# Start offsets of SBUF tiles: small tiles move to one filled pool, and every large tile begins at a multiple of 512 bytes

## The chip, the core and the metric

One core of a Trainium2 chip runs the whole layer. The metric is the device time of one execution in microseconds (us). The program is one straight list of instructions for each engine, so every execution issues the same work in the same order.

## What is computed

One layer of a hybrid encoder on x of shape (1, 512, 1024) in float32, with hidden width 2816 in the two feed-forward halves:

```
x = x + 0.5 * swiglu(rmsnorm(x, ffn1_norm_g), ffn1_w_gate, ffn1_w_up, ffn1_w_down)
h = rmsnorm(x, mix_norm_g)
proj = h @ w_in                                   # 1024 -> 3072
y_hy = hyena_mixer(proj[..., :1536], ...)         # gates and two long convolutions
y_at = dilated_attention_mixer(proj[..., 1536:])  # 8 heads of 64
y = concatenate([rmsnorm(y_hy, ...), rmsnorm(y_at, ...)])
x = x + y @ w_out
x = x + 0.5 * swiglu(rmsnorm(x, ffn2_norm_g), ffn2_w_gate, ffn2_w_up, ffn2_w_down)
return rmsnorm(x, final_norm_g)
```

## The kernel before

**The matmuls.** Activations lie transposed in SBUF: 128 channels on the partitions, the 512 tokens along each partition. So a tile of 128x512 float32 takes 2048 bytes of each partition, and a block of weights of 128x128 takes 512. To keep float32 accuracy at the rate of the type float32r, each operand is split in a high part, rounded to float32r, and a low part, the rest. `mm3` then issues three matmuls for each block, at lines 146, 147 and 148: high times high, high weights times low activations, low weights times high activations. The weights are the stationary operand, the 512 tokens the moving one. Where float32 itself is multiplied (transposes with `ident`, the products of the attention weights with v, the sums over `ones`), a matmul leaves two records in the trace.

**The tiles by name.** Weights arrive in `wr` by DMA (128x1024, 4096 bytes of each partition), ScalarE (ACT) rounds them to `wh` (line 188) and VectorE (DVE) subtracts to `wl` (line 194). The moving operand is `xh`, `xl` for gate and up (output `pgu`), for the input projections (`pp`), and the stationary one for v (`pv`, where `wh`, `wl` move); `gh`, `gl` for the down projection (`pd`); the tiles named `yg` for the output projection (`pw`). Some early projections take their weights from tiles named `we` instead of `wh`. The filters use `ftabh`, `ftabl` as stationary and `fh`, `fl` as moving operand (`pf`); the Hyena part uses `zh`, `zl` against `ftab` (`pfw`) and `Sh`, `Sl` against `itab` (`pbk`) at 256 columns each.

**The order.** Stages follow each other: FFN 1 (with the filter work woven in, to about 402 us), the mixer (projections, Hyena, attention, output projection, to about 670 us), FFN 2. Inside a stage, streams of work with planned costs are merged by the class `Merge` into one fixed order. Weights are loaded two blocks ahead by SP's queue.

**Where tiles lie.** A pool takes a stretch of each partition, and its tiles stand in it in the order of their first use, each tag times its number of buffers. Every tile is padded to a multiple of 32 bytes. Pools opened with `side="right"` are stacked down from the top. In the built program x0 begins at byte 16512 of the partition, that is 32 x 512 + 128. Counting on from there gives, modulo 512:

| tiles | pool | start modulo 512 |
|---|---|---|
| x0 to x7 | wp | 128 |
| ones | wp | 0 |
| wr, wh, wl, ident, xh, xl, ssq, sq, rb | wp, after cols, eps, ones and warm | 32 |
| z, u, gh, gl; ur, zh, zl, X (yg among them), Sh, Sl | f1, f2; m1, after std and rc | 160 |
| we, qk, v, yh; ftab, itab; fh, fl and most filter tiles | mid; tp; fl (right side) | 480 |

Here cols takes 352 bytes, eps and warm 32 each, and the two buffers each of std and rc take 128 together. The right side ends 32 bytes below the end of the partition.

Of the kernel before, what the change touches and what calls it, by code (L numbers as in the profile page):

```python
# [11 lines left out]
F32 = mybir.dt.float32  # L12
# [6 lines left out]
P = 128  # L19
# [16 lines left out]
NG1, NGM, NGH, NGA, NG2, NGF, NCW, NCB = 0, 8, 16, 20, 24, 32, 40, 76  # L36
NCOL = 88
WR, WB, HQ, SB, UC, ZB, X1B, UR = 2, 3, 3, 3, 3, 3, 3, 3
TWO_PI = 2.0 * math.pi


# [13 lines left out]
def on_p(cost, lag=0.4, **need):  # L55
    return "P", cost, lag, need


def on_v(cost, lag=None, **need):
    return "V", cost, lag, need  # L60


def on_a(cost, lag=0.2, **need):
    return "A", cost, lag, need
# [176 lines left out]
class SumSq:  # L241
# [38 lines left out]
    def rstd_cols(self, n, lag, res, m, ev):  # L280


        g, nc = self.g, self.g.nc
        yield on_v(0.0, lag)
        parts = self.sums()
        yield on_p(0.9 * len(parts), ps=1)
        pc = psum(g, "pc")
        for b in range(4):
            for i, t in enumerate(parts):
                nc.tensor.matmul(pc[:, b:b + 1], t[:, b * P:(b + 1) * P], g.ones[:, 0:1],  # L290
                                 start=i == 0, stop=i == len(parts) - 1)
        yield on_v(0.5, 0.4)
        std = g.wp.tile([P, 4], F32, tag="std", name="std", bufs=2)
        nc.scalar.activation(std, pc[:, 0:4], AF.Sqrt, bias=g.eps, scale=1.0 / n)
        rc = g.wp.tile([P, 4], F32, tag="rc", name="rc", bufs=2)
        nc.vector.reciprocal(rc, std)
        res["rc"] = rc
        m.free(ps=1)
        yield on_p(0.9, ps=1)
        pb = psum(g, "pb")  # L300
        for b in range(4):
            spread(g, pb[:, b * P:(b + 1) * P], rc[:, b:b + 1], P)
        yield on_a(0.7)
        res["rb"] = g.wp.tile([P, S], F32, tag="rb", name="rb", bufs=1)
        nc.scalar.copy(res["rb"], pb)
        m.free(ps=1)
        m.fire(ev)


def spread(g, ps, col, n):  # L310

    g.nc.tensor.matmul(ps, col.to_broadcast([P, n]), g.ident, start=True, stop=True)


def psum(g, name):
    return g.ps.tile([P, S], F32, tag="ps", name=name)
# [85 lines left out]
def split_tab(g, pool, name, src):  # L402
    nc = g.nc
    raw = g.wp.tile([P, 1024], F32, tag="wr", name="tabraw", bufs=WR)
    nc.sync.dma_start(raw, src)
    hi = pool.tile([P, 1024], F32R, tag=name + "h", name=name + "h", bufs=1)
    lo = pool.tile([P, 1024], F32R, tag=name + "l", name=name + "l", bufs=1)
    nc.scalar.activation(hi, raw, AF.Copy)
    nc.vector.tensor_tensor(out=lo, in0=raw, in1=hi.bitcast(F32), op=ALU.subtract)
    return hi, lo  # L410


def sin_layer(g, pool, out, ps, n, b, fr):
# [5 lines left out]
    magic = 12582912.0  # L419
    nc.vector.tensor_scalar(out=t[:n], in0=a[:n], scalar1=1.0 / TWO_PI, scalar2=magic,  # L420
                            op0=ALU.mult, op1=ALU.add)
    nc.vector.tensor_scalar_add(t[:n], t[:n], -magic)
    c1 = 6.28125
    c2 = float(np.float32(np.round((TWO_PI - c1) * 2.0 ** 21) / 2.0 ** 21))
    c3 = float(np.float32(TWO_PI - c1 - c2))
    for c in (c1, c2, c3):
# [7 lines left out]
def filters(g, m, pool, tpool, a, start, done):  # L434
# [3 lines left out]
    yield on_v(2.3, 6.0)  # L438
    g.ftab = split_tab(g, tpool, "ftab", a["ftab"])
    g.itab = split_tab(g, tpool, "itab", a["itab"])  # L440
    fq = pool.tile([P, 4], F32, tag="fq", name="fq", bufs=1)
    nc.sync.dma_start(fq, a["fcol"])
    zt = pool.tile([P, S], F32, tag="fr", name="zt", bufs=1)
# [659 lines left out]
def body(ctx: ExitStack, tc: tile.TileContext, a: dict, out: bass.AP):  # L1103
    nc = tc.nc
    g = Ctx()
    g.nc, g.tc = nc, tc
    pool = lambda n, **k: tc.tile_pool(name=n, bufs=1, **k)
    over = dict(reuse_waits="tile")
    g.ps = ctx.enter_context(tc.tile_pool(name="ps", bufs=8, space=PSUM))
    g.wp = ctx.enter_context(pool("wp"))  # L1110
    dp = ctx.enter_context(pool("dp", space=DRAM))
    g.hdram = [dp.tile([5, 2, P, 2 * CW], F32, tag=f"hd{o}", name=f"hdram{o}") for o in range(2)]
# [2 lines left out]
    n1w = len(f1)  # L1115
    g.w = Weights(g, f1 + mixer_weights(a) + f2)
    g.x = [g.wp.tile([P, S], F32, tag=f"x{d}", name=f"x{d}") for d in range(DT)]
    g.cols = g.wp.tile([P, NCOL], F32, tag="cols", name="cols")
    g.eps = g.wp.tile([P, 1], F32, tag="eps", name="eps")
    nc.vector.memset(g.eps, EPS)  # L1120
    g.ones = g.wp.tile([P, P], F32, tag="ones", name="ones")
    nc.vector.memset(g.ones, 1.0)
    g.warm = warm = g.wp.tile([P, 1], F32, tag="warm", name="warm")
    nc.scalar.activation(warm, g.eps, AF.Silu)
    ps = psum(g, "warm")
    for _ in range(NWARM):
# [5 lines left out]
        if d == 1:  # L1132
            g.w.start()
    g.w.load(1)
    g.ident = g.wp.tile([P, P], F32, tag="ident", name="ident")
    make_identity(nc, g.ident)


# [2 lines left out]
    with pool("f1", **over) as fp:  # L1141
# [29 lines left out]
        st = left.enter_context(pool("st", **over))  # L1171

        m.spawn(filters(g, m, flp, tp, a, nev, fdone), 0.5)
        m.run(until=fdone)
        right2.close()
# [11 lines left out]
    with pool("m1", **over) as hp:  # L1187
# [13 lines left out]
        def squares():  # L1201

            yield wait(at.xev)
            for d in range(DT):
                yield on_v(0.0, 1.4)
                with tc.issue_after(g.rounded.ins):
                    ss2.add(g.x[d])
# [10 lines left out]
    with pool("f2", **over) as fp:  # L1218
        ss3 = SumSq(g)
        n2, nev = {}, Event()  # L1220
        gain = lambda d: g.cols[:, NGF + d:NGF + d + 1]
        sq = {}
        pc = []

        def done2(d):
            ss3.add(g.x[d])
            nc.scalar.activation(g.x[d], g.x[d], AF.Copy, scale=gain(d))
            if d == DT - 4:
                nc.scalar.activation(warm, ss3.acc[:, 0:1], AF.Sqrt)

        def tail(d, th, ps):

            hs = slice(th * CW, (th + 1) * CW)
            x = g.x[d][:, hs]
            if d == DT - 2:
                yield on_p(0.4, 0.0, ps=1)
                pc.append(psum(g, "pc"))
                for b in range(2):
                    bs = slice((2 * th + b) * P, (2 * th + b + 1) * P)
                    nc.tensor.matmul(pc[th][:, b:b + 1], ss3.acc[:, bs], g.ones[:, 0:1],  # L1240
                                     start=b == 0, stop=False)
            yield on_v(0.35)
            nc.vector.scalar_tensor_tensor(out=x, in0=ps[:, 0:CW], scalar=0.5, in1=x,
                                           op0=ALU.mult, op1=ALU.add)
            m.free(ps=1)
            yield on_v(0.0, 0.4)
            sq[d] = g.wp.tile([P, S], F32, tag="sq", name="sq", bufs=2)
            nc.scalar.activation(sq[d][:, 0:CW], x, AF.Square)
            yield on_p(0.3)
            for b in range(2):  # L1250
                nc.tensor.matmul(pc[th][:, b:b + 1], sq[d][:, b * P:(b + 1) * P],
                                 g.ones[:, 0:1], start=False, stop=d == DT - 1 and b == 1)
            if d < DT - 1:
                return
            yield on_v(0.3, 0.6)
            std = g.wp.tile([P, 4], F32, tag="std", name="std", bufs=2)
            nc.scalar.activation(std[:, 0:2], pc[th][:, 0:2], AF.Sqrt, bias=g.eps, scale=1.0 / D)
            rc = g.wp.tile([P, 4], F32, tag="rc", name="rc", bufs=2)
            nc.vector.reciprocal(rc[:, 0:2], std[:, 0:2])
            yield on_p(0.5, 0.2, ps=1)  # L1260
            pb = psum(g, "pb")
            for b in range(2):
                spread(g, pb[:, b * P:(b + 1) * P], rc[:, b:b + 1], P)
            for c in range(DT // 2):
                yield on_v(0.7)
                o = g.wp.tile([P, 2, CW], F32, tag="xh", name="o", bufs=DT)
                for i in range(2):
                    e = 2 * c + i
                    if e < DT - 2:
                        nc.vector.tensor_tensor(out=o[:, i], in0=g.x[e][:, hs], in1=pb[:, 0:CW], op=ALU.mult)  # L1270
                    else:
                        nc.vector.scalar_tensor_tensor(out=o[:, i], in0=g.x[e][:, hs], scalar=gain(e),
                                                       in1=pb[:, 0:CW], op0=ALU.mult, op1=ALU.mult)
                (nc.sync if c % 2 else nc.scalar).dma_start(
                    out[2 * c:2 * c + 2, :, hs].rearrange("d p s -> p d s"), o)
            m.free(ps=2)

        m.spawn(ffn(g, m, fp, at.x2, n2, nev, done2, tail), 1)

        def norm2():  # L1280
            yield from squares()
            yield from ss2.rstd(D, L2, n2, m, nev)

        m.spawn(norm2(), 0)
        m.run()
# [114 lines left out]
```

## Time and profile before

| | |
|---|---|
| median of 3 runs | 1048.6 us (1047.63 to 1049.46) |
| the profiled execution's own time | 1048.07 us |
| its span, first to last instruction | 1046.3 us |
| PE (TensorE matmul) busy | 1032.0 us, 99% of the span |
| DVE (VectorE) busy | 604.5 us, 58% |
| ACT (ScalarE) busy | 402.5 us, 38% |
| mean share of the 16 DMA engines | 33.3% on the main queue |
| granted TensorE clock, mean | 0.995 of 2.4 GHz |

PE's records overlap: a matmul's record lasts 0.39 us, but the next one begins some 0.23 us after it. The pace of a stream of matmuls is therefore read from start to start, or from the number of records in a long stretch, and not from the mean duration of a record.

### The profile page before, as it was taken

The numbers are of one execution on the slowest core, as the hardware profiler recorded it, in microseconds if no ns is written. First come the engines' busy times: TensorE is split into PE (matmuls) and PEld (weight loads), VectorE is DVE, ScalarE is ACT, GpSimd is POOL, SyncE is SP. The second block draws the span as 40 slices with busy tenths as digits, with TensorE's granted clock in tenths as the row PEclk, the third lists the DMA queues.
The fourth block names the chain that finished last, engine by engine and source line by source line (L and its number), as shares of the span: only waits on it lengthen the run. The fifth ranks groups of instructions, "written<-read, shape, count | busy, mean of one in ns | idle before, by whom it ended". The sixth has DMA issues, their size and how long they took to land.

```text
span 1046.3 us, 12667 instructions
## 1 busy us (share of the span) xinstructions
PE 1032.0 (99%) x5012; PEld 844.7 (81%) x5012; DVE 604.5 (58%) x834; ACT 402.5 (38%) x594; POOL 45.9 (4%) x37
## 2 busy tenths in 40 slices
PE   9999999999999999999998999999999999999997
PEld 7877888888888888888886778888888888888886
DVE  5676646554676444887999744764453235444332
ACT  6433432233334332344347874543232213333341
POOL 4000000000000111000000000210000000000010
PEclk9999999999999999999999999999999999999998
DMA  6333423533255222234435311233322332332222
GB/s 216 129 124 106 126 91 118 174 98 104 91 170 171 92 90 91 66 114 143 143 105 186 122 42 61 81 101 101 101 89 93 101 100 86 96 101 101 93 69 81
DMA packets 43513, 114.25 MB, mean 109 GB/s; under 512 B 5082, under 2 KB 12314, under 8 KB 43453
## 3 DMA queue, kind: packets, MB, share of 16 engines
q1 hardware_dynamic: 41644, 111.30, 33.3%
q10 hardware_dynamic: 1808, 2.14, 0.6%
q8 instruction: 39, 0.64, 0.3%
q14 instruction: 22, 0.17, 0.1%
HBM read 106.08 MB, written 7.34 MB: 108 GB/s over the span
## 4 chain that ended last, share of the span: by engine, by line
PE 96%; DVE 2%; ACT 1%; issue 1%; DMA 1%; SPq 0%; DVEq 0%; ACTq 0%
PE pgu L146 15%; PE pgu L147 15%; PE pgu L148 15%; PE pd L146 8%; PE pd L148 8%; PE pd L147 8%; PE pp L146 3%; PE pp L148 3%; PE pp L147 3%; PE pw L146 2%; PE pw L148 1%; PE pw L147 1%; PE po L1008 1%; PE ppt L996 1%; PE pqk L1039 1%; PE pv L146 1%
## 5 line engine op out<-in xcount | busy, mean ns | idle before, releaser
L188 ACT ACTIVATE wh<-wr 128x1024 fp32r<-128x1024 f32 x159 | 168.5, 1060 | 411.9 <-PE pgu L147 143.1
L146 PE MATMUL pgu<-xh,wh 128*128 128x512 f32 x704 | 275.4, 391 | 0.4 <-ACT wh L580 0.4
L147 PE MATMUL pgu<-xl,wh 128*128 128x512 f32 x704 | 274.4, 390 | 0.3 <-DVE xl L236 0.3
L148 PE MATMUL pgu<-xh,wl 128*128 128x512 f32 x704 | 274.5, 390 | 0.1
L194 DVE TENSOR_TENSOR wl<-wr,wh 128x1024 fp32r<-128x1024 f32 x159 | 198.1, 1246 | 114.3 <-ACT wh L188 110.0
L146 PEld LDWEIGHTS pgu<-xh,wh 128*128 128x128 f32 x704 | 132.2, 188 | 31.0 <-issue 2.9
L147 PEld LDWEIGHTS pgu<-xl,wh 128*128 128x128 f32 x704 | 132.1, 188 | 29.6 <-DVE xl L236 1.4
L148 PEld LDWEIGHTS pgu<-xh,wl 128*128 128x128 f32 x704 | 132.1, 188 | 28.3 <-DVE wl L581 0.4
L146 PE MATMUL pd<-gh,wh 128*128 128x512 f32 (+1 forms) x374 | 143.2, 383 | 0.0
L147 PE MATMUL pd<-gl,wh 128*128 128x512 f32 (+1 forms) x374 | 142.7, 382 | 0.0
L148 PE MATMUL pd<-gh,wl 128*128 128x512 f32 (+1 forms) x374 | 142.7, 382 | 0.0
L256 POOL TENSOR_TENSOR ssq<-ssq,sq 128x512 f32<-128x512 f32 x31 | 45.2, 1457 | 975.5 <-ACT sq L252 974.6
L331 DVE TENSOR_TENSOR u<-pgu,rb 128x512 f32<-128x512 f32 x44 | 30.3, 690 | 97.3 <-PE pgu L148 97.3
L147 PEld LDWEIGHTS pd<-gl,wh 128*128 128x128 f32 x374 | 70.3, 188 | 15.1
L148 PEld LDWEIGHTS pd<-gh,wl 128*128 128x128 f32 x374 | 70.3, 188 | 15.0
L146 PEld LDWEIGHTS pd<-gh,wh 128*128 128x128 f32 x374 | 70.3, 188 | 15.0
L329 DVE TENSOR_TENSOR z<-pgu,rb 128x512 f32<-128x512 f32 x44 | 30.4, 691 | 60.6 <-PE pgu L148 60.5
L146 PE MATMUL pp<-xh,wh 128*128 128x512 f32 x128 | 50.0, 391 | 0.0
L147 PE MATMUL pp<-xl,wh 128*128 128x512 f32 x128 | 49.9, 390 | 0.0
L148 PE MATMUL pp<-xh,wl 128*128 128x512 f32 x128 | 49.8, 389 | 0.0
L343 DVE SCALAR_TENSOR_TENSOR x<-pd,x 128x512 f32<-128x512 f32 x30 | 20.7, 690 | 42.7 <-PE pd L148 42.6
L336 ACT ACTIVATE gh<-u 128x512 fp32r<-128x512 f32 x44 | 27.7, 632 | 24.2 <-DVE u L333 23.8
(207 smaller groups left out, 1189.3 us busy)
## 6 DMA issues: line engine op xcount, KB each, us to landing
wr<-w1u SPq DMA_DIRECT2D x22, 512.0 KB, 3.4
wr<-w1d SPq DMA_DIRECT2D x22, 512.0 KB, 3.4
wr<-w2g SPq DMA_DIRECT2D x22, 512.0 KB, 3.4
wr<-w2u SPq DMA_DIRECT2D x22, 512.0 KB, 3.4
wr<-w2d SPq DMA_DIRECT2D x22, 512.0 KB, 3.4
wr<-w1g SPq DMA_DIRECT2D x21, 512.0 KB, 3.4
wr<-win SPq DMA_DIRECT2D x16, 512.0 KB, 3.4
pe<-negb SPq DMA_DIRECT2D x32, 256.0 KB, 3.2
```

The lines of the kernel that those rows point to most:

```text
L146: nc.tensor.matmul(ps, lh, rh, start=start, stop=False)
L147: nc.tensor.matmul(ps, lh, rl, start=False, stop=False)
L148: nc.tensor.matmul(ps, ll, rh, start=False, stop=stop)
L188: self.g.nc.scalar.activation(self.hi[i], self.raw[i], AF.Copy)
L194: self.g.nc.vector.tensor_tensor(out=self.lo[i], in0=self.raw[i], in1=self.hi[i].bitcast(F32), op=ALU.subtract)
L256: g.nc.gpsimd.tensor_tensor(out=self.acc, in0=self.acc, in1=sq, op=ALU.add)
L329: nc.vector.tensor_tensor(out=z, in0=pg, in1=rb, op=ALU.mult)
L331: nc.vector.tensor_tensor(out=u, in0=pu, in1=rb, op=ALU.mult)
L336: nc.scalar.activation(hi, u, AF.Copy)
L343: nc.vector.scalar_tensor_tensor(out=g.x[d], in0=ps, scalar=0.5, in1=g.x[d], op0=ALU.mult, op1=ALU.add)
L996: nc.tensor.transpose(ts[e][:, js], pes[e][:, js], g.ident)
L1008: nc.tensor.matmul(po[e * HD:(e + 1) * HD, b * P:(b + 1) * P], self.mx.v[j][:, h * HD:(h + 1) * HD], tt[e][:, j * P:(j + 1) * P], start=j ...
```

## The change

A new pool `sp` is opened ahead of `wp`, and its first tile is `fill`, 88 float32 on each partition, which nothing writes or reads. The small tiles cols, eps, warm, std and rc move into `sp`. `ident` is allocated right behind `ones`, while the instructions that fill it stay where they were. On the right side, `fillr` (120 float32, also unused) is allocated in `tp` behind the tables.

```
+SMALL = 88
 class SumSq, rstd_cols, and the tail of FFN 2:
-        std = g.wp.tile([P, 4], F32, tag="std", name="std", bufs=2)
+        std = g.sp.tile([P, 4], F32, tag="std", name="std", bufs=2)
-        rc = g.wp.tile([P, 4], F32, tag="rc", name="rc", bufs=2)
+        rc = g.sp.tile([P, 4], F32, tag="rc", name="rc", bufs=2)
 filters:
     g.itab = split_tab(g, tpool, "itab", a["itab"])
+    tpool.tile([P, 120], F32, tag="fill", name="fillr")
 body:
+    g.sp = ctx.enter_context(pool("sp"))
+    g.sp.tile([P, SMALL], F32, tag="fill", name="fill")
     g.wp = ctx.enter_context(pool("wp"))
-    g.cols = g.wp.tile([P, NCOL], F32, tag="cols", name="cols")
-    g.eps = g.wp.tile([P, 1], F32, tag="eps", name="eps")
+    g.cols = g.sp.tile([P, NCOL], F32, tag="cols", name="cols")
+    g.eps = g.sp.tile([P, 1], F32, tag="eps", name="eps")
     g.ones = g.wp.tile([P, P], F32, tag="ones", name="ones")
-    g.warm = warm = g.wp.tile([P, 1], F32, tag="warm", name="warm")
+    g.ident = g.wp.tile([P, P], F32, tag="ident", name="ident")
+    g.warm = warm = g.sp.tile([P, 1], F32, tag="warm", name="warm")
...
-    g.ident = g.wp.tile([P, P], F32, tag="ident", name="ident")
     make_identity(nc, g.ident)
```

Counted out: 16512 + 352 (fill) + 352 (cols) + 32 (eps) + 32 (warm) + 64 (std) + 64 (rc) = 17408 = 34 x 512, where `wp` now begins. `wp` then holds only tiles of whole multiples of 512 bytes, so f1, m1 and f2 begin at such a multiple too; they lie 352 bytes higher than before. On the right side everything lies 480 bytes lower: the tables begin at 212480 = 415 x 512, and `mid` at 179712 = 351 x 512.

## Rows read from the trace of the kernel before

**Rows 1.** The page's first part: busy us, share of the span, instructions.
```profile
PE 1032.0 (99%) x5012; PEld 844.7 (81%) x5012; DVE 604.5 (58%) x834; ACT 402.5 (38%) x594; POOL 45.9 (4%) x37
```

**Rows 2.** Waits of PE: total us, times, longest; first and last of eight.
```profile
PE po L1008 <- ACT pt L1002: 1.9, 1, 1.9
...
PE pgu L147 <- DVE xl L236: 0.3, 1, 0.3
```

**Rows 3.** Stretches: length; busy of PE, PEld, DVE, ACT, POOL (records); clock, DMA share, GB/s.
```profile
10.00:402.00 392.00, 391.77 (x1692) 316.58 (x1693) 234.29 (x295) 147.52 (x196) 18.75 (x13) 1.00 0.38 123
...
500.00:572.00 72.00, 68.92 (x390) 57.20 (x388) 71.28 (x119) 36.12 (x67) 1.27 (x1) 1.00 0.47 149
...
655.00:1022.00 367.00, 367.00 (x1618) 301.30 (x1617) 166.50 (x193) 116.55 (x142) 18.30 (x12) 1.00 0.29 94
```

**Rows 4.** PE alone: a stretch of pgu, then one of pd; records, clock, DMA.
```profile
860.00:965.00 105.00, 105.00 (x465) 1.00 0.30 96
975.00:1015.00 40.00, 40.00 (x173) 1.00 0.29 93
```

**Rows 5.** Timeline of PE in pd: start us, length us, instruction.
```profile
800.01 0.39 PE L146 MATMUL pd<-gh,wh 128*128 128x512 f32 x1
800.24 0.40 PE L147 MATMUL pd<-gl,wh 128*128 128x512 f32 x1
800.48 0.39 PE L148 MATMUL pd<-gh,wl 128*128 128x512 f32 x1
```

**Rows 6.** Timeline of PE: pw, 20 steps apart.
```profile
655.17 0.39 PE L147 MATMUL pw<-yg,wh 128*128 128x512 f32 x1
...
659.82 0.40 PE L146 MATMUL pw<-yg,wh 128*128 128x512 f32 x1
```

**Rows 7.** Timeline of PE: pp with we, 10 steps apart.
```profile
401.62 0.39 PE L147 MATMUL pp<-xl,we 128*128 128x512 f32 x1
...
403.91 0.39 PE L148 MATMUL pp<-xh,we 128*128 128x512 f32 x1
```

**Rows 8.** Timeline of PE: pf to the next pgu, 3 steps apart.
```profile
116.86 0.40 PE L146 MATMUL pf<-fh,ftabh 128*128 128x512 f32 x1
...
117.57 0.39 PE L146 MATMUL pgu<-xh,wh 128*128 128x512 f32 x1
```

**Rows 9.** Timeline of PE: pfw of 256 columns, 11 steps apart.
```profile
424.16 0.28 PE L146 MATMUL pfw<-zh,ftabh 128*128 128x256 f32 x1
...
425.46 0.28 PE L148 MATMUL pfw<-zh,ftabl 128*128 128x256 f32 x1
```

**Rows 10.** Chain that ended last, float32 pieces: start us, us, records.
```profile
586.80 0.87 PE ppt L996 x8
...
692.25 0.86 PE pb L270 x2
```

**Rows 11.** Groups of PE: one of the three lines of each class, with its count.
```profile
L146 PE MATMUL pgu<-xh,wh 128*128 128x512 f32 x704 | 275.4, 391 | 0.4 <-ACT wh L580 0.4
...
L147 PE MATMUL pd<-gl,wh 128*128 128x512 f32 x330 | 130.4, 395 | 0.0
...
L146 PE MATMUL pp<-xh,wh 128*128 128x512 f32 x128 | 50.0, 391 | 0.0
...
L146 PE MATMUL pw<-yg,wh 128*128 128x512 f32 x64 | 26.4, 415 | 0.0
...
L146 PE MATMUL pp<-xh,we 128*128 128x512 f32 x32 | 12.9, 402 | 0.0
L146 PE MATMUL pv<-wh,xh 128*128 128x512 f32 x32 | 12.8, 401 | 0.0
...
L148 PE MATMUL pfw<-zh,ftabl 128*128 128x256 f32 x32 | 9.0, 281 | 0.0
```

**Rows 12.** DMA queues: packets, MB, share of 16 engines.
```profile
q1 hardware_dynamic: 41644, 111.30, 33.3%
```

**Rows 13.** Last work on the filter tiles: ns min/median/max, first and last start us.
```profile
L556 DVE TENSOR_TENSOR ho<-Ha x8: 681/686/693, 185.0 to 314.2; 128x512 f32<-128x512 f32 x8
```

More of the change, by code (lines that the diff above doesn't have):

```diff
@@ L1255, in tail @@
             yield on_v(0.3, 0.6)
-            std = g.wp.tile([P, 4], F32, tag="std", name="std", bufs=2)
+            std = g.sp.tile([P, 4], F32, tag="std", name="std", bufs=2)
             nc.scalar.activation(std[:, 0:2], pc[th][:, 0:2], AF.Sqrt, bias=g.eps, scale=1.0 / D)
-            rc = g.wp.tile([P, 4], F32, tag="rc", name="rc", bufs=2)
+            rc = g.sp.tile([P, 4], F32, tag="rc", name="rc", bufs=2)
             nc.vector.reciprocal(rc[:, 0:2], std[:, 0:2])
```

## The prediction

> **What bounds the kernel now.** I read the page's shares first, then the waits of PE, then the stretches by stage, and last the starts of single matmuls. PE is busy for 1032.0 of 1046.3 us [rows 1], and its eight waits run from 1.9 down to 0.3 us [rows 2]. So nothing hands PE work too late: in the two FFN stretches, 392 and 367 us long, it never rests, at a granted clock of 1.00 (the 2.4 GHz level), while DVE is busy 60% and 45% of the time and the DMA engines 38% and 29% [rows 3]. One stretch is different: from 500 to 572 us DVE is busy for 71.28 of 72 us, and there a faster PE would wait for it [rows 3]. So the time goes down only if the pace of the matmuls themselves changes, and this change touches nothing but addresses.
>
> The pace is the thing to look at. 512 columns at 2.4 GHz, one to a clock, take 213.3 ns. In FFN 2, 465 records of pgu touch a stretch of 105 us; a record lasts 0.39 us, so their starts spread over 105.39 us, 226.6 ns from one to the next [rows 4]. The same for pd: 40.39 us over 173, 233.5 ns [rows 4]. Both streams are unbroken, have the same shape and weights tiles, and cost 13 and 20 ns more than their columns. In pd the steps are uneven, 230 and 240 ns in turn [rows 5]. What differs between the two classes is where the moving operand starts: xh and xl at 32 modulo 512 bytes, gh and gl at 160. The other classes fit an influence of the address. pw, at 160 too, takes 4.65 us for 20 steps, 232.5 ns [rows 6]. pp with its weights at 480 instead of 32 takes 2.29 us for 10, 229 ns [rows 7]. pf, with both operands at 480, takes 0.71 us for 3, about 237 ns there [rows 8].
>
> The second clue is float32. A record of ppt (128 columns, two clocks to a column, 106.7 ns) takes 0.87/8 = 108.8 ns, one of pb (512 columns, 426.7 ns) 0.86/2 = 430 ns: 2.1 and 3.3 ns over their columns, though ident and ssq also start at 32 modulo 512 [rows 10]. So a fixed cost of a matmul is 2 to 3 ns, and the other 10 to 17 ns show up only where a column is read on every clock. At 256 columns pfw takes 1.30 us for 11 steps, 118.2 ns against 106.7 [rows 9]: the excess of 11.5 ns grows with the columns (20 ns for pd's 512 at the same offset). A cost that grows with what is streamed, differs with the start address, and is absent when the stream runs at half the rate looks like a price of reading off some boundary.
>
> **The change part by part.** *No instruction is added or removed.* fill and fillr are never touched; std, rc, eps, warm and cols keep their order and their buffers; ident is only allocated earlier. Cost: nothing, bounded by nothing on either side unless an address matters.
>
> *Pools that follow each other in the same bytes.* f1, m1 and f2 rise by 352 bytes together and the right side falls by 480, so m1's last tiles now overlap other tiles of the filter pool than before. The filters' last work starts at 314.2 us [rows 13], and m1 begins after 402 us, so no wait can come of it. Between m1 and mid 192 bytes stay free (179520 to 179712).
>
> *DMA.* The weights land on other offsets. The queue fills 33.3% of the engines [rows 12], and PE waits for no DMA [rows 2]. Even a tenth more or less on each transfer is covered by loading two blocks ahead; the price is 0, with 0.3 us either way for the first loads before PE has work.
>
> *DVE, ACT, POOL.* Their operands move too. A gain or loss there lies under PE, except in the 72 us where DVE is full. If DVE changed by 1% there, that is 0.7 us; I take 0.
>
> *TensorE's operands.* This is the one part with weight. All moving and stationary operands of the large matmuls go to 0 modulo 512. No matmul at one column to a clock with such a start exists in this trace, so the price is bounded: from below by the fixed 2.7 ns of the float32 records, 216.0 ns for 512 columns and 109.4 for 256; from above by the worst class seen in a long stream, 233.5 ns. I take 216.0, because the excess depends on the address and 0 is where any boundary of a power of two up to 512 is met. By class, three lines each [rows 11]:
>
> - pgu: 2112 matmuls x (226.6 - 216.0) = 22.4 us
> - pd: 990 x 17.5 = 17.3 us
> - pp and pv: 480 x 10.6 = 5.1 us
> - pw: 192 x 16.5 = 3.2 us
> - pp with we: 96 x 13 = 1.2 us
> - pfw: 96 x 8.8 = 0.8 us
>
> Together 50.0 us. From this goes what DVE keeps back from 500 to 572 us: 72 x 10.6/226.6 = 3.4 us. pf, pbk and the narrow pd are left out of the sum; they have the same sign and widen the low end by some 4 us. So 1048.07 - 46.6 = 1001.5 us for an execution like the profiled one, and with 0.5 us between it and the median, 1002 us.
>
> The Trainium skill speaks against this. Its page "SBUF — State Buffer", under "Specifications (TRN2)", gives the cachelines of SBUF as 16 bytes, with a penalty for crossing to a new one. All offsets here, 32, 128, 160 and 480, are multiples of 16, so by that rule nothing was misaligned and the sum would be 0, 1048.6 us. The trace does not bear the rule out as the whole story, since pgu and pd differ by 7 ns. The page "TensorE: Matmul & The Clock Gate", under "Back-to-back issue gap", gives N/2.4 + 2.5 ns for a warm stream, 215.8 ns here; this trace's pgu shows 226.6 instead.
>
> **The rivals.** *Only the distance counts.* The excess may come from two reads in PE, weights and moving operand, that hinder each other by their distance: 0 modulo 512 in pgu (226.6), 128 in pd and pw (233.5 and 232.5), 64 in pp with we (229). After the change every distance is 0, as in pgu now. Gain: 990 x 6.9 + 192 x 5.9 + 96 x 2.4 = 8.1 us, so 1040.5 us. For it: pgu is the best class and has distance 0. Against it: pf has distance 0 as well and is slower than pgu, though its three matmuls stand alone between others.
>
> *It doesn't do what it says.* The excess belongs to this type at full rate, and what separates pd from pgu is its work on the other engines. Then the time stays at 1048.6 us. Against it: pp with we and pp run the same work and differ.
>
> *Slower: a common start makes reads collide.* With weights and moving operand on the same boundary every time, every block could begin on the same part of SBUF. pf, the one class with equal offsets beside the boundary, is the slow row that speaks for it; pgu, with equal offsets too, speaks against. If pgu, pp and pv fall to pd's pace and the others keep it, that costs 2592 x 6.9 + 192 x 1 + 96 x 4.5 = 18.5 us: 1067 us. The point from which it decides is a common pace of 228.7 ns, the mean over the counts above; anything slower than that ends behind the kernel before.
>
> **How the numbers follow.** Excess gone, wholly or by half and more: 0.60, likeliest time 1002 us, its own range 992 (the left-out classes and no loss to DVE) to 1025 us (half of 46.6 us gained). Distance alone: 0.20, 1040.5 us. No effect: 0.08. Slower: 0.12, up to 1067 us. A change within 0.2%, 2 us, can't be told from none on this kernel. The first two cases are faster: 0.80; same 0.08; slower 0.12. The range runs from 990 to 1044 us and leaves the last two cases out, 0.20 together.
>
> **What the profile of the changed kernel would show.** Right: the same instruction counts on every engine; in a long stretch of pgu or pd one record each 216 ns, with no alternation in pd and no difference between the two; pfw near 109 ns; float32 records as before; DVE still full near 500 to 570 us; no new wait on PE. Distance alone: pd falls to pgu's 226.6 ns and pgu stays. No effect: both keep their pace. Collision: pgu at or above 230 ns. I would be wrong in size if the pace stops between, say at 220 ns, or if a faster PE meets weights that are not ready (waits of PE on wl, L194, in FFN 2), which DVE's 45% makes unlikely.

## The result and the profile after

The changed kernel takes 1040.95 us (median of 6 runs, 1038.31 to 1041.51), the kernel before 1048.63 us (1047.63 to 1049.46). The ratio is 0.9919, 95% interval 0.9906 to 0.9933: faster by 0.8%, 7.7 us. The forecast was 46.6 us. So the direction was right and the size was not; the time is that of the rival "only the distance counts" (1040.5 us), which had a chance of 0.20. The six executions of the changed kernel fall in two groups, 1038.31 and 1038.46 us at a mean granted clock of 0.997 and 0.998, and 1040.93 to 1041.51 us at 0.995 and 0.996; the profiled one is the fastest of them.

The shares of the page hardly moved: PE still sets the time, with the same number of instructions on every engine as in [rows 1].

```profile
PE 1023.0 (99%) x5012; PEld 844.1 (81%) x5012; DVE 604.2 (58%) x834; ACT 402.3 (39%) x594; POOL 46.0 (4%) x37
```

The waits of PE, first and last of eight, answer to [rows 2]; the last, 0.2 us, is the only new one.

```profile
PE po L1010 <- ACT pt L1004: 1.9, 1, 1.9
...
PE pb L313 <- DVE rc L297: 0.2, 1, 0.2
```

The pace is where the change shows. These are the stretches of pgu and pd in FFN 2 (length, busy, records), as in [rows 4], and pd's single starts, as in [rows 5].

```profile
860.00:965.00 105.00, 105.00 (x465) 1.00 0.29 98
970.00:1005.00 35.00, 35.00 (x156) 1.00 0.28 91
```

```profile
800.04 0.39 PE L147 MATMUL pd<-gh,wh 128*128 128x512 f32 x1
800.27 0.39 PE L148 MATMUL pd<-gl,wh 128*128 128x512 f32 x1
800.49 0.39 PE L149 MATMUL pd<-gh,wl 128*128 128x512 f32 x1
800.72 0.39 PE L147 MATMUL pd<-gh,wh 128*128 128x512 f32 x1
```

pgu has exactly the 465 records it had before: 105.39/465 = 226.6 ns, unchanged. pd went from 233.5 to 35.39/156 = 226.9 ns, and its steps no longer alternate as in [rows 5] (the starts are printed in steps of 10 ns, and 230, 220 and 230 is what 227 becomes in them). pd has taken pgu's pace; neither came near 216. The output projection answers to [rows 6], 20 steps from 648.85 to 653.39:

```profile
648.85 0.39 PE L147 MATMUL pw<-yg,wh 128*128 128x512 f32 x1
...
653.39 0.39 PE L149 MATMUL pw<-yg,wl 128*128 128x512 f32 x1
```

That is 4.54 us, 227 ns after 232.5. pp with we, ten steps as in [rows 7], took 2.26 us, 226 ns after 229:

```profile
396.19 0.39 PE L148 MATMUL pp<-xl,we 128*128 128x512 f32 x1
...
398.45 0.39 PE L149 MATMUL pp<-xh,we 128*128 128x512 f32 x1
```

The 256-column class went the other way: 11 steps of pfw take 1.31 us, 119.1 ns after the 118.2 of [rows 9].

```profile
419.40 0.28 PE L147 MATMUL pfw<-zh,ftabh 128*128 128x256 f32 x1
...
420.71 0.28 PE L149 MATMUL pfw<-zh,ftabl 128*128 128x256 f32 x1
```

By stage, from the first matmul of the next one, in the two profiled executions (1048.07 and 1038.31 us; the one of the changed kernel is 2.6 us under its median): FFN 1 ends at 400.69 before and 395.96 now, 4.7 us earlier; the mixer takes 269.6 and 267.9 us, 1.7 less; FFN 2 to the end of the span 376.0 and 372.7, 3.3 less. FFN 2 is explained by its 462 wide pd: 462 x 6.6 = 3.0 us. FFN 1 has 528 of them, 3.5 us; most of the rest came from the filter matmuls and from pgu beside them. In equal parts of the woven stretch, 224 records of pgu kept PE busy for 53.36 us before and 52.89 us now (length, then busy by engine for pgu alone; the kernel before, then the changed one):

```profile
240.00:300.00 60.00, 53.36 (x224) 42.19 (x225) 6.23 (x9) 1.00 0.34 109
```

```profile
238.00:297.00 59.00, 52.89 (x224) 41.92 (x224) 6.23 (x9) 1.00 0.33 111
```

The 1.7 us of the mixer cannot be put down to addresses. In the profiled execution of the kernel before, the granted clock was 0.79 over 8 us, that is its lower level (1.2 GHz) for some 3.4 us, just behind a stretch in which PE worked 0.29 of 2 us; in that of the changed kernel it was 1.00 over the whole mixer (the kernel before, two stretches, then the changed one). Half the clock for 3.4 us is worth up to 1.7 us, an estimate from these rows. It may also be why these two executions lie 9.8 us apart and the medians only 7.7.

```profile
570.00:572.00 2.00, 0.29 (x2) 1.00 0.60 216
572.00:580.00 8.00, 7.90 (x54) 0.79 0.10 28
```

```profile
396.00:664.00 268.00, 263.54 (x1610) 1.00 0.34 107
```

### The profile page after: what moved, and what is told of

Its sections match the earlier page's. It is cut to its first block, busy times and chain, and to the rows that moved or that the text cites. A ratio compares the mean times of both kernels' runs of the same rounds, so it can differ in the third digit from the quotient of the medians.

```text
span 1036.5 us, 12667 instructions
## 1 busy us (share of the span) xinstructions
PE 1023.0 (99%) x5012; PEld 844.1 (81%) x5012; DVE 604.2 (58%) x834; ACT 402.3 (39%) x594; POOL 46.0 (4%) x37
## 4 chain that ended last, share of the span: by engine, by line
PE 96%; DVE 2%; ACT 1%; issue 1%; DMA 0%; ACTq 0%; SPq 0%; DVEq 0%
PE pgu L148 15%; PE pgu L147 15%; PE pgu L149 15%; PE pd L147 8%; PE pd L148 8%; PE pd L149 8%; PE pp L147 3%; PE pp L149 3%; PE pp L148 3%; PE pw L147 2%; PE pw L149 1%; PE pw L148 1%; PE po L1010 1%; PE ppt L998 1%; PE pqk L1041 1%; PE pv L147 1%
```

## The experiments

The theory to test against my forecast: a float32r matmul of 512 columns costs 226.7 ns at best, and more when the start of its moving operand, less the start of its weights, is not 0 modulo some number of bytes ("distance"). The rival is the forecast's own idea ("boundary"): the multiple of 512 itself counts. Paces below come from records in long stretches, as above: (length + 0.39 us) / records. One record more or less is 1.0 ns in a stretch of 55 us, 1.5 in one of 35 and 2.6 in one of 20. Where a finer difference matters, the text gives the mean of all steps from start to start in the trace, and says so. Where no ratio is given, the time is that of a single execution, and the changed kernel's own six are spread over 3.2 us; such times support an argument only where they differ by more.

### The distance mended without any boundary

The kernel before, with 384 unused bytes ahead of f1, m1 and f2:

```
+        fp.tile([P, 96], F32, tag="fill", name="pad")     # f1 and f2; hp.tile in m1
```

> The kernel before, with one unused tile of 384 bytes at the start of the pools f1, m1 and f2: their tiles start at 32 modulo 512 as the weights do, nothing starts at a multiple of 512, the right side stays at 480. Theory 'distance' (what counts is the start of the moving operand relative to the weights): pd falls from 233.3 to 226.7 ns from start to start, pw from 232.5 to about 228, pgu stays at 226.7; 990 x 6.6 + 192 x 4.5 = 7.4 us, so about 1041 us, the time of the changed kernel. Theory 'boundary' (the multiple of 512 itself counts): nothing is on it, so no gain, 1048.6 us.

1042.25 us, ratio to the kernel before 0.9944 (0.9925 to 0.9962). Stretches of pgu and pd:

```profile
860.00:965.00 105.00, 105.00 (x465) 1.00 0.31 98
975.00:1010.00 35.00, 35.00 (x156) 1.00 0.27 90
```

226.6 and 226.9 ns, as in the changed kernel, while no weight and no activation of the large matmuls starts at a multiple of 512. The gain is there without the boundary.

### Every tile at 160

The changed kernel with other sizes of the two fill tiles:

```
-SMALL = 88
+SMALL = 128
-    tpool.tile([P, 120], F32, tag="fill", name="fillr")
+    tpool.tile([P, 80], F32, tag="fill", name="fillr")
```

> The changed kernel with both fill tiles resized so that every large tile, left and right, starts at 160 modulo 512, where gh and gl started before. 'Distance': every distance is still 0, so pgu and pd stay at 226.7 ns and the time at 1041 us. 'Boundary' (a moving operand that starts at 160 pays for it): pgu, pp, pv and pd all near 233 ns, 3600 matmuls x 6.6 ns = 24 us more, about 1065 us.

1041.56 us, ratio 0.9935 (0.992 to 0.9951), again with pgu and pd at one pace:

```profile
860.00:965.00 105.00, 105.00 (x465) 1.00 0.29 95
975.00:1010.00 35.00, 35.00 (x156) 1.00 0.27 91
```

160 is the very offset at which gh and gl cost 233.5 ns before. With the weights at 160 too they cost 226.9. "Boundary" is out.

### Distances 128 and 256

The changed kernel, with f1 shifted by 128 bytes and f2 by 256:

```
+        fp.tile([P, 32], F32, tag="fill", name="pad")     # f1
+        fp.tile([P, 64], F32, tag="fill", name="pad")     # f2
```

> The changed kernel with gh and gl shifted by 128 bytes against the weights in FFN 1 and by 256 in FFN 2. 'Distance': pd in FFN 1 goes back to 233.3 ns, the pace of distance 128 before, and 528 x 6.6 = 3.5 us are lost there; in FFN 2 the pace shows whether the period is 512 (then not 226.7) or 256 (then 226.7). pgu stays at 226.7 in both. 'Boundary': also a loss in FFN 1, the same in FFN 2.

1042.25 us. pd in FFN 1, then in FFN 2:

```profile
345.00:400.00 55.00, 55.00 (x237) 1.00 0.31 98
975.00:1010.00 35.00, 35.00 (x156) 1.00 0.29 91
```

55.39/237 = 233.7 ns at 128, back to the old pace in a kernel where all else is aligned; 226.9 at 256. So a distance of 256 bytes costs no more than none.

### A different offset for every pair

Each gh/gl pair got its own offset by slicing or by odd tile sizes:

```
+            o = OFFS[ft] // 4
+            hi = fp.tile([P, S + P], F32R, tag=f"gh{ft}", name="gh", bufs=1)[:, o:o + S]
+            lo = fp.tile([P, S + P], F32R, tag=f"gl{ft}", name="gl", bufs=1)[:, o:o + S]
```

> The changed kernel with each of the eleven gh/gl pairs at an offset of its own: 0, 32, 64 to 320 in FFN 1; 352, 384, 416, 448, 480, 16, 8, 4, 48, 240, 0 in FFN 2. Both theories: the pace of three matmuls on one pair depends on the offset, lowest at 0. 'Distance' expects a smooth or periodic curve between 226.7 and 238 ns; if some offset lies below 226.7, there is a version faster than the changed kernel; if offsets that are a multiple of 64 are all cheap, 512 is more than is needed.

1046.09 us, and no curve: pd takes 40.39/174 = 232.1 ns in the stretch below.

```profile
800.00:840.00 40.00, 40.00 (x174) 1.00 0.29 93
```

That mean decides nothing, since most of these offsets turn out slow by themselves (below). The single pairs say more (mean of all their steps in the trace): the pairs at 0 take 231.1 (offset 0) and 230.6 ns (offset 256) in FFN 1 and 230.1 in FFN 2, the others 231.4 to 235.1. So the pairs at 0 are the fastest of their stage, as expected, but only by 0.3 to 1.3 ns, and they do not come down to 226.7: three matmuls at a good distance between bad ones do not reach the pace of a stream that keeps it. For that reason the run gives no pace of a single distance.

### Six more distances, held constant

The changed kernel with unused tiles ahead of xh and ahead of f1 and f2, so that each class keeps one distance:

```
+        g.wp.tile([P, 16], F32, tag="pad", name="pad")    # ahead of xh: 64 bytes (24: 96)
+        fp.tile([P, 32], F32, tag="fill", name="pad")     # f1: to 192 (16: to 160)
+        fp.tile([P, 120], F32, tag="fill", name="pad")    # f2: to 32 (32: to 224)
```

> The changed kernel with unused tiles that set the distance of the moving operand from the weights, modulo 512, to 64 for pgu, pp and pw, to 192 for pd in FFN 1 and to 32 for pd in FFN 2. 'Distance with period 256' (0 and 256 cost 226.7 ns, 128 costs 233.3): paces between these, near 230 ns at 64 and 192 and near 228 at 32; some 8 us longer than the changed kernel. A pace under 226.7 anywhere would fall outside this theory and make a faster kernel.

> The same with distance 96 for pgu, pp and pw, 160 for pd in FFN 1, 224 for pd in FFN 2. 'Distance with period 256': near 231.5 ns at 96 and 160, near 228 at 224; some 14 us longer than the changed kernel. Equal paces at 96 and 160 and at 32 and 224 would mean that the sign of the distance doesn't count.

1053.48 and 1064.25 us. Three stretches each: pd in FFN 1, pgu, pd in FFN 2; first distances 192, 64, 32, then 160, 96, 224.

```profile
345.00:400.00 55.00, 55.00 (x237) 1.00 0.29 96
870.00:965.00 95.00, 95.00 (x417) 1.00 0.29 96
980.00:1015.00 35.00, 35.00 (x152) 1.00 0.30 97
```

```profile
350.00:405.00 55.00, 55.00 (x237) 1.00 0.29 95
875.00:965.00 90.00, 90.00 (x387) 1.00 0.30 95
990.00:1025.00 35.00, 35.00 (x152) 1.00 0.27 91
```

The smooth curve that was expected is wrong too: 32 already costs 35.39/152 = 232.8 ns, as much as 128 within the resolution, and 64 alone lies between, at 95.39/417 = 228.8 (192: 233.7, 160: 233.7, 96: 233.6, 224: 232.8). The sign counts: 64 and 192, which is -64, differ, and in the first of these kernels pv, where xh is the stationary operand and the distance is -64, takes 233.4 ns against 228.9 of pp at 64 (mean of all steps). The 256-column matmuls follow another rule. In four of the eight groups of pfw at distance 64, 11 steps take 1.25 us, 113.6 ns, against 119.1 at 0:

```profile
493.42 0.28 PE L147 MATMUL pfw<-zh,ftabh 128*128 128x256 f32 x1
...
494.67 0.28 PE L149 MATMUL pfw<-zh,ftabl 128*128 128x256 f32 x1
```

The other four groups of the same kernel take 117.7 to 117.9 ns at the same distance, and so do all eight in the first experiment, whose pfw also has distance 64 (32 less 480, modulo 256). What sets the pace at 256 columns stays open.

### Distances below 32

High and low part of a pair lie in one tile, sliced 16 bytes (FFN 1) or 8 bytes (FFN 2) from its start:

```
+        o = 4 if tail is None else 2
+        gp = fp.tile([P, 2 * S + 64], F32R, tag="gh", name="gh", bufs=HALF)
+        hi, lo = gp[:, o:o + S], gp[:, o + S:o + 2 * S]
```

> The changed kernel with gh and gl at a distance of 16 bytes from the weights in FFN 1 and of 8 bytes in FFN 2 (modulo 256), pgu at 0. At distances of 0, 32, 64, 96, 128, 160, 192 and 224 the paces were 226.7, 233.3, 229.2, 233.4, 233.3, 234.1, 233.3 and 233.3 ns. If distances count in steps of 32 bytes, 8 and 16 cost what 0 does, 226.7; if every distance but 0 and 64 is slow, 233 ns for both, 990 x 6.6 = 6.5 us more than the changed kernel, 1047 us. A pace below 226.7 would show that the 13.3 ns over the columns are in part an address cost too.

1044.49 us. pd in FFN 1 and FFN 2:

```profile
343.00:398.00 55.00, 55.00 (x239) 1.00 0.29 94
790.00:845.00 55.00, 55.00 (x238) 1.00 0.31 96
```

231.8 ns at 16 and 232.7 at 8, one record apart; the mean of all steps is 231.7 and 232.3. So 16 bytes off is nearly as bad as 128, and nothing lies under 226.7. The time is 3.5 us over the changed kernel's median where 6.5 were expected. That is no sign of cheap distances: this execution had a granted clock of 0.998, and against the changed kernel's two at 0.997 and 0.998 it is 6.0 to 6.2 us longer.

### What the 13.3 ns at distance 0 are

First, fewer weights beside the same stream. In FFN 1's gate and up, only 64 of 128 columns are loaded for two matmuls of three, or for 22 of 24, so half of the outputs lack these products (the first of the two kernels):

```
+                        nc.tensor.matmul(ps[0:64], lh[:, 0:64], rl, start=False, stop=False)
+                        nc.tensor.matmul(ps[0:64], ll[:, 0:64], rh, start=False, stop=False)
```

> The changed kernel, where in FFN 1's gate and up the second and third matmul of each block (but the last block of a sum) load 64 of 128 columns of weights and write half of the outputs; so the small corrections of the other half are left out. The moving stream is the same. Theory 'load' (the 13.3 ns that every float32r matmul costs over its columns at distance 0 come from the weights read beside the stream): the steps beside a 64-column load fall by about half of it, to some 220 ns, and FFN 1 gets about 616 x 6 ns = 4 us shorter. Theory 'stream' (they belong to streaming float32r itself): all steps stay at 226.7 ns and the time at 1041 us.

> The changed kernel, where in FFN 1's gate and up all matmuls of a sum but its first and its last load 64 of 128 weight columns, so 22 narrow loads follow each other; left out are these products for half of the outputs. 'Load' (half the weight bytes beside the stream, half the excess): 220 ns from start to start in FFN 1's pgu against 226.7 in FFN 2's. 'Stream': 226.7 in both. A third reading, 'pattern' (the cost hangs on how loads and stream meet in time, not on the bytes of a load): some other steady value, above 226.7 as well as below.

1043.58 and 1042.53 us. The stretches of pgu in FFN 1 and, with whole loads, FFN 2, in the second of the two:

```profile
35.00:55.00 20.00, 20.00 (x88) 12.12 (x87) 5.00 (x8) 1.00 0.29 102
860.00:960.00 100.00, 100.00 (x443) 82.82 (x442) 12.69 (x19) 1.00 0.28 95
```

20.39/88 = 231.7 ns with half loads, 226.6 with whole ones (in the first of the two 20.39/89 = 229.1). Stretches of 20 us are too short to tell these two from each other; the mean of all steps of pgu in FFN 1 is 229.8 ns in the second and 229.9 in the first, against 227.0 there in the changed kernel. Halving the weights made the stream slower by some 3 ns. "Load", in the form that the cost follows the bytes loaded, falls; "stream" alone expected no change and falls as well. A half load does not take half the time, though: by the lines above it lasts 12.12/87 = 139 ns, a whole one 82.82/442 = 187. What is left is the third reading, that the cost hangs on how stream and load meet in time; it is left over, not shown.

Second, the same matmuls with bfloat16 parts (the operands of FFN, projections and output projection are less precise), once with all tiles as in the changed kernel and once where the kernel before had them:

```
+BF = mybir.dt.bfloat16
-        hi = g.wp.tile([P, S], F32R, tag="xh", name="xh", bufs=DT)
+        hi = g.wp.tile([P, 2 * S], BF, tag="xh", name="xh", bufs=DT)[:, 0:S]
...
```

> The changed kernel with the high and low parts of the FFN, projection and output weights and activations held in bfloat16 instead of float32r (three products as before, less precise operands), still starting at multiples of 512 bytes; filters, Hyena tables and attention stay float32r. Half the bytes for stream and weights. 'Load' and 'stream' both expect that the excess of 13.3 ns nearly goes: 216 ns from start to start, 3870 x 10.7 = 41 us less where PE is the bound, about 1003 us. If the pace stays at 226.7 ns the excess has nothing to do with bytes read.

> The kernel with high and low parts in bfloat16, timed (the same text as in the look before: FFN, projection and output operands less precise). 998 us, ratio to the kernel before 0.952, faster than the changed kernel by 4%.

> The same bfloat16 parts with the tiles where the kernel before had them (wp at 32, f1 and m1 at 160, right side at 480 modulo 512). 'Distance' holds for 4-byte operands read at one column to a clock: with half the bytes the start should not matter, every class at 216 ns, the time within 2 us of the bfloat16 kernel at multiples of 512. If a bfloat16 stream also pays for the distance, pd and pw are slower here by 4 to 7 ns, 5 to 8 us in all.

At multiples of 512 a first execution took 997.92 us; the median of four more is 998.66 us, ratio to the kernel before 0.9528 (0.9512 to 0.9544), and with the old offsets it is 998.76 us, 0.9527 (0.9513 to 0.9541). pd in the kernel with the old offsets, where its distance is still 128, and then at distance 0:

```profile
961.89 0.38 PE L147 MATMUL pd<-gh,wh 128*128 128x512 bf16 x1
...
962.97 0.38 PE L149 MATMUL pd<-gh,wl 128*128 128x512 bf16 x1
```

```profile
961.81 0.38 PE L149 MATMUL pd<-gl,wh 128*128 128x512 bf16 x1
...
962.89 0.38 PE L148 MATMUL pd<-gh,wh 128*128 128x512 bf16 x1
```

Five steps in 1.08 us in both, 216 ns. With two bytes to a column the 13.3 ns shrink to 2.7, and a distance of 128 costs nothing. The loads change too: one of 128 columns lasts 98 ns in bfloat16 and 188 in float32r.

## Why the prediction was wrong

**The reading of what bounds the kernel was right.** PE's pace moved, DVE, ACT and DMA stayed as they were, no wait of more than 0.2 us came in, and none came of the pools that follow each other in the same bytes. The small edits were rightly put at 0. The range of 990 to 1044 us holds the measured time only because it was drawn wide enough to take in the rival; the forecast inside it was missed by 39 us. Its own low end, 992 us, does not follow from its terms either: 1002 less 3.4 and 4 us is 994.6.

**The step that failed is the price of a matmul at 0 modulo 512.** I took 216.0 ns for 512 columns "because the excess depends on the address and 0 is where any boundary of a power of two up to 512 is met". Part of the excess does depend on an address, but on the difference of two, moving operand less weights, with 256 as good as 0. With both at 160, or both at 32, the pace is the same 226.6 to 226.9 ns as with both at 0. Since pgu, pp and pv had distance 0 before, nearly all of their 27.5 of the 50.0 us of the sum could not come, and pd, pw and pp with we gained 6.6, 5.5 and 3 ns instead of 17.5, 16.5 and 13.

**The clue from float32 was misread.** It is true that the excess is absent where a column takes two clocks. I concluded that all of it is an address cost that can go. The two parts have different ends: 0 to 7 ns hang on the distance, 13.3 ns stay at every start tried. The bfloat16 kernel reaches the 216 ns that I forecast, so the floor was the right one for two-byte operands, at a time (998.66 us) 50 us under the kernel before; with float32r, the addresses alone gave 7.7.

**The evidence against the distance was misread.** pf, with equal offsets of 480, was slower than pgu in [rows 8], and I counted that against the distance. The three steps that I read, 237 ns, were a slow sample: the mean of all such steps in that trace is 231.4. Even so, pf and pgu both had distance 0 there, so their own distances do not explain the difference. What differs is the place, 480 for the filters and 32 for FFN 1. Where filter matmuls stand among pgu (200 to 300 us, mean of all steps), pgu takes 228.4 ns in the kernel before and 228.5 in the first experiment, which leaves the filters at 480; it takes 226.7 in the changed kernel and with every tile at 160, where filters and FFN start alike. In the kernel before, the steps of pgu stay above 226.7 for some ten matmuls behind each group of pf, up to 234 ns at the third. So here a stream kept its pace only while the class next to it started at the same place as well. In the trace each load of weights begins together with the matmul before its own, so at a change of class one pair's moving operand runs beside the other pair's weights. That would make it the distance again; it fits, but no run tests it by itself.

**The rivals.** "Only the distance counts" was right in what sets the pace and, at 1040.5 us against 1040.95, in its size; that two reads hinder each other, its reason, is not shown by any run. "Slower" has its grain of truth in the 256-column class, which lost 1 ns. "It doesn't do what it says" is out, since the time fell by 7.7 us; but the 512 has no part in it, and no tile needs to lie on a multiple of it.

**The Trainium skill.** By the Trainium skill's page "SBUF — State Buffer", section "Specifications (TRN2)", with cachelines of 16 bytes, nothing was misaligned and the change would have had no effect; measured are 7.7 us, and a distance of 16 bytes costs 231.8 ns against 226.7, so that rule does not account for what the change did. The Trainium skill's page "TensorE: Matmul & The Clock Gate" gives, under "Back-to-back issue gap", N/2.4 + 2.5 ns at the full clock, an estimate of 215.8 ns for 512 columns; the section calls it the gap of a single isolated matmul, which I passed over when I took it for a stream. It agrees with the 216 ns of the bfloat16 stream here, and not with the 226.7 of float32r.

**What stays open** is what the 13.3 ns at distance 0 are. They shrink to 2.7 with two-byte operands, where stream and load both have half the bytes, and grow by some 3 ns when the loads are halved. That fits stream and load hindering each other, but no run here separates the two reads: in every trace each float32r matmul has a load of its own beside the stream before it.

## What to carry to other kernels

In a stream of float32r matmuls, start the moving operand and the weights at the same place modulo 256 bytes, and give all classes that alternate in one stream the same place: 3% of the pace hung on it here, and one unused tile ahead of a pool mends it. Before pricing what an address can give back, look for the class that already has the good value: pgu already stood at distance 0, and its 226.6 ns was the floor to forecast. If the precision allows three bfloat16 products in place of three float32r ones, that is worth six times as much (4.7%), and the old offsets and the new gave the same time.

## What the runs showed of the hardware that was not expected

- Pace from start to start, float32r, 512 columns, by distance modulo 256 (mean of all steps of the class in its stage; distances over 256 were tried only as 256 itself and in mixed streams): 0: 226.7 ns; 8: 232.3; 16: 231.7; 32: 233.3; 64: 228.9; 96: 233.3; 128: 233.3; 160: 234.1; 192: 233.3; 224: 233.3. At 256 columns: 119 at 0, and at 64 either 113.4 or 117.8 from group to group.
- The pace belongs to the stream: with another distance every three matmuls, those at 0 take 230 to 231 ns, not 226.7. Behind a group of matmuls whose tiles start elsewhere, a stream needs some ten matmuls to come back to its pace.
- Loading 64 instead of 128 weight columns beside the same stream took 229.8 ns from start to start, 3 more; a load of 64 columns lasted 135 to 139 ns, one of 128 columns 188.
- bfloat16 takes 216 ns at distance 0 and at 128.
